# Moving three pieces of work around the choice of experts: 1/rms before the last rows, the first weight splits behind the choice, the first expert's tokens before the slot table

## The chip, the cores and the metric

One Trainium2 chip, one of its cores. The metric is device time in microseconds for one execution of the whole program (a mixer block, a mixture of experts, a second block with two feed-forward nets and two attentions). The change touches the stretch between the mixer's last projection and the first expert.

## The reference, cut to what matters

512 tokens of width 1024. After the mixer, `h = rms_norm(x)` goes into a mixture of 32 experts in 4 groups; each token takes two experts of one group, and each expert is a gated net of inner width 512.

```python
def hierarchical_moe(h, w_rg, b_rg, w_re, b_re, w_gate, w_up, w_down):
    g_logits = xt @ w_rg + b_rg                      # 4 groups
    g_sel = jnp.argmax(g_logits, axis=-1)
    g_w = softmax(g_logits)[g_sel]
    e_logits = (xt @ w_re + b_re)[group g_sel]       # 8 experts of that group
    top_v, top_i = lax.top_k(e_logits, 2)
    e_w = jax.nn.softmax(top_v, axis=-1) * g_w
    expert_id = g_sel * 8 + top_i
    ...                                              # tokens sorted by expert
    y = (jax.nn.silu(xb @ w_gate[e]) * (xb @ w_up[e])) @ w_down[e]
    out = out.at[sorted_tok].add(y * sorted_w)
```

## The kernel before, in words

Everything is float32. A dense product is made of three passes over operands that are split into a high and a low half: `mm3` (lines 257 to 259) multiplies low by high, high by low, and high by high. The split is `hilo`: ScalarE copies the rounded half (line 203), VectorE subtracts it from the source (line 204). Weights arrive by DMA into buffers of the pool `t8` (16 buffers of 1 MB), are split in pieces of 128x1024 into the pool `wp` (3 buffers), and a `t8` buffer is free for the next transfer once both of its pieces are split.

**Order.** A scheduler places each engine's instructions from the order of the program text and its own estimates; on its engine each then runs in the order written down. `keep_in_program_order` forbids it to move the marked instruction past others. The names in rows are tiles: `ps` is a PSUM bank, `t` any buffer of the shared pools, `wh` and `wl` the halves of a weight piece, `x` the residual stream.

**Into the experts.** `router` (line 556) returns `step(k)`, called for each of the 8 feature blocks of the new `x`: it squares the block into the sum `hsq` (lines 215 and 217), adds the block's product with the router's weights to the logits (line 573), scales and transposes the block (lines 576 and 579) and copies it to token rows (line 581). `moe` (line 661) then takes 1/rms of `hsq` (`rstd`: column sums by TensorE at line 286, line 315, the square root at line 268 and its refinement on VectorE), writes the token rows to `hrow` in DRAM, and chooses groups and experts (lines 693 to 727).

**Two fixed experts first.** 25 positions hold one or two experts each; positions 0 and 1 are always experts 0 and 1 (`NFIXED`), all later ones are ordered by how many tokens an expert got. For experts 0 and 1 the token lists are found without a table (`fixed`, lines 747 to 752) and their rows gathered from `hrow` on the GpSimd queue (line 1042); `fixed2` (line 758) adds their combine weights. All other experts need the slot table: VectorE computes each assignment's row (lines 785 to 794, the tile `dest`), eight indirect DMAs on the GpSimd queue scatter the assignments to `table` in DRAM (line 804), seven more read it back as `tabb`, `tab2` and `tab3` (lines 824 to 832), and the next gathers use those.

**The loop.** `features(n)` transposes gathered rows (line 1052 for a large position, with a split after it; line 954 for one or two small experts), `up` and `down` are the expert's products, `turn` the transpose between them, and the gather for position n+2 is issued while position n is worked on. Position 2 is a pair of small experts, so its rows come through `tab3` and its transposes are line 954. The raw weights of positions 0 and 1 are loaded ahead of the choice; those of the other positions are addressed by the ordered list `order`, through register loads on the sync queue (line 634) that precede its DMAs (line 238).

Of the kernel before, what the change touches and what calls it, by code (L numbers as in the profile page):

```python
# [7 lines left out]
F32 = mybir.dt.float32  # L8
# [3 lines left out]
ALU = mybir.AluOpType  # L12
# [4 lines left out]
T, D = 512, 1024  # L17
NT = T // 128
ND = D // 128
# [13 lines left out]
NFIXED, NBIG, NSMALL, CAP = 2, 6, 18, 64  # L33
# [4 lines left out]
SPLITS = 2  # L38
# [14 lines left out]
SEQ = sequence()  # L53
# [22 lines left out]
class Blocks:  # L76


    def __init__(self, tiles, n, w=512):
        self.tiles, self.n, self.w, self.per = tiles, n, w, 2048 // w  # L80
# [37 lines left out]
class Net:  # L118
    def __init__(self, tc, ctx, A, out):
        self.tc, self.nc, self.A, self.out, self.ctx = tc, tc.nc, A, out, ctx  # L120
        nc = self.nc
        ec = ctx.enter_context
        self.own = None
        self.const = ec(tc.tile_pool(name="const", bufs=1))
        self.p8 = ec(tc.tile_pool(name="p8", bufs=16))
        self.p4 = ec(tc.tile_pool(name="p4", bufs=4))
        self.p2 = ec(tc.tile_pool(name="p2", bufs=5))
        self.wp = ec(tc.tile_pool(name="wp", bufs=3))
        self.sm = ec(tc.tile_pool(name="sm", bufs=2))
        self.pp = ec(tc.tile_pool(name="pp", bufs=8, space=PSUM))  # L130
        self.dr = ec(tc.tile_pool(name="dr", bufs=1, space=DRAM))
        c = self.const
        self.x = c.tile([128, ND, T], F32, name="x")
        self.vec = c.tile([128, NV], F32, name="vec")
        nc.scalar.dma_start(self.vec, A["vec"])
        self.cc = c.tile([128, NC_], F32, name="cc")
        nc.scalar.dma_start(self.cc, A["cc"])
        self.ident = self.cc[:, C_ID:C_ID + 128]
        self.ones = c.tile([128, 128], F32, name="ones")
        nc.vector.memset(self.ones, 1.0)  # L140
        self.table = self.dr.tile([ROUNDS * 128 * NE, 4], I32, name="table")
        self.ordd = self.dr.tile([1, NE], I32, name="ordd")
        self.hrow = self.dr.tile([T, D], F32, name="hrow")
        self.pay = c.tile([128, NT, 2, 4], I32, name="pay")
        self.br = c.tile([128, NG + NE], F32, name="br")
        self.order = c.tile([128, NE], I32, name="order")
        self.payf = c.tile([128, NT, NFIXED, 4], F32, name="payf")
        self.payi = c.tile([128, NT, 2], F32R, name="payi")
        self.g12 = c.tile([128, ND], F32, name="g12")
        o1, o2 = VOFF["norm_final_g"], VOFF["g_ffn1_2"]  # L150
        nc.vector.tensor_tensor(self.g12, self.vec[:, o1:o1 + ND], self.vec[:, o2:o2 + ND], op=ALU.mult)
# [48 lines left out]

    def hilo(self, hi, lo, src):
        nc = self.nc
        nc.scalar.copy(hi, src)  # L203
        nc.vector.tensor_tensor(lo, src, hi.bitcast(F32), op=ALU.subtract)  # L204

    def half(self, hi, lo, src, g):

# [346 lines left out]
    def router(self):  # L554

        nc, W = self.nc, NG + NE
        self.root_table()
        x4 = self.t8([128, 2, D])
        nc.gpsimd.memset(x4, 0.0)
        self.xts = [x4[:, b, :] for b in range(2)]  # L560
        nc.gpsimd.dma_start(self.br, self.A["b_router"].partition_broadcast(128))
        wr = self.t2(ND * W).rearrange("p (k w) -> p k w", k=ND)
        nc.gpsimd.dma_start(wr, self.A["w_router"])
        for k in range(ND):
            nc.gpsimd.tensor_scalar(wr[:, k], wr[:, k], self.v("norm_ffn_g", k), None, op0=ALU.mult)
        self.lg = lg = self.ps()
        self.hsq = acc = self.t2()
        self.rows_x = rows = [self.t4([128, D]) for _ in range(NT)]

        def step(k):  # L570
            self.square(acc, self.x[:, k, :], k == 0)
            for i in range(NT):
                nc.tensor.matmul(lg[:, i * W:i * W + W], self.x[:, k, i * 128:i * 128 + 128], wr[:, k, :],
                                 start=k == 0 and i == 0, stop=k == ND - 1, skip_group_check=True)
            t = self.t2()
            nc.scalar.mul(t, self.x[:, k, :], self.v("norm_ffn_g", k))
            p = self.ps()
            for i in range(NT):
                nc.tensor.transpose(p[:, i * 128:i * 128 + 128], t[:, i * 128:i * 128 + 128], self.ident)
            for i in range(NT):  # L580
                nc.scalar.copy(rows[i][:, k * 128:k * 128 + 128], p[:, i * 128:i * 128 + 128])
        return step
# [78 lines left out]
    def moe(self):  # L661
        nc, A, tc = self.nc, self.A, self.tc
        mul, add, sub = ALU.mult, ALU.add, ALU.subtract
# [3 lines left out]
        ur, er = two[:, 0:128], two[:, 128:256]  # L667
        nc.gpsimd.tensor_copy(ur, self.cc[:, C_U:C_U + 128])
        nc.gpsimd.tensor_copy(er, self.ones)
        rt = self.rstd([self.hsq], D, "rtok")  # L670
        hrow, table, pay, payf = self.hrow, self.table, self.pay, self.payf
        for i in range(NT):
            nc.scalar.dma_start(hrow[i * 128:i * 128 + 128, :], rows[i])
# [5 lines left out]
        four = self.t2().rearrange("p (a i e) -> p a i e", i=NT, e=NE)  # L679
        where = {"Em": 0, "o1": 1, "o2": 2, "P": 3}  # L680

        def small(nm, w, dt=F32):
            return four[:, where[nm]] if nm in where else self.keep(nm, [128, NT, w], dt)
# [49 lines left out]
        for i in range(NT - 1):  # L733
            n = NT - i
            mm(rk[:, 32 * i + 32:160].rearrange("p (a e) -> p a e", e=NE), er,
               O[:, i:i + 1, :].to_broadcast([128, n, NE]), start=False, stop=i == NT - 2, skip_group_check=True)
        rk3 = rk[:, 0:128].rearrange("p (i e) -> p i e", e=NE)
# [16 lines left out]
        def fixed2(e):  # L754

            p = self.ps()
            for i in range(NT):
                mm(p[:, 0:2], sels[e].bitcast(F32)[:, i, :], payf[:, i, e, 0:2], start=i == 0, stop=i == NT - 1)
            nc.vector.tensor_copy(tabs[e].bitcast(F32)[:, 2:4], p[:, 0:2])
# [3 lines left out]
        rank, order, less = self.ranks(cn)  # L763
# [11 lines left out]
        nc.vector.tensor_tensor(pf[0], o1[:, :, fx], bc(ds, NFIXED), op=mul)  # L775
        nc.vector.tensor_tensor(pf[0], pf[0], pf[1], op=add)
        nc.vector.tensor_copy(pf[1], rt.rearrange("p (i o) -> p i o", o=1).to_broadcast([128, NT, NFIXED]))
        for e in range(NFIXED):
            fixed2(e)
        P = small("P", NE)  # L780
        rowr, row, tmp = P, Em, P

        def all4(t):
            return t.rearrange("p (o e) -> p o e", o=1).to_broadcast([128, NT, NE])
        nc.vector.tensor_tensor(rowr, rk3, all4(less), op=add)
        nc.vector.scalar_tensor_tensor(rowr, rowr, 127.5, all4(less), op0=ALU.is_ge, op1=mul)
        nc.vector.tensor_tensor(rowr, rowr, rk3, op=add)
        nc.vector.scalar_tensor_tensor(row, rowr, float(NE), all4(rank), op0=mul, op1=add)
# [13 lines left out]
        for i in range(NT):  # L802
            for j in range(2):
                ins = nc.gpsimd.indirect_dma_start(
                    table, bass.IndirectOffsetOnAxis(ap=dest[:, i, j:j + 1], axis=0),
                    pay[:, i, j, :], None, bounds_check=NR - 1, oob_is_err=False)
# [23 lines left out]
        for h in range(4):  # L830
            n = NE - NSMALL - h % 2
# [10 lines left out]
            else:  # L842
                self.gather(self.xts[n % 2][0:CAP], tabs[p][0:CAP])

        def features(n):
            xt = self.xts[n % 2]
            return self.expert_x(xt) if SEQ[n][0] < NBIG else self.small_x(xt)

        def up(n, xT, ys=()):
            unit = SEQ[n]  # L850
            tab = tabs[unit[0]]

            def also(k):
                if ys and k % 2:
                    for b in (k - 1, k):
                        self.add_block(ys, b)
            if unit[0] < NBIG:
                return self.expert_up(self.split_next, xT, tab, also)
            return self.small_up(unit, xT, tab, also)
# [4 lines left out]
        def down(n, aT):  # L864
# [3 lines left out]
            y = self.expert_down(self.split_next, aT, tab) if unit[0] < NBIG else self.small_down(unit, aT, tab)  # L868
            self.presplit(self.wnext + SPLITS)
            return [(t, sel) for t in y]  # L870
        a, ys = up(0, features(0)), ()
        xT = features(1)
        for n in range(NU - 2):
            aT = turn(n, a)
            gather(n + AHEAD)
            a = up(n + 1, xT, ys)
            xT = features(n + 2)
            ys = down(n, aT)
        aT, before = turn(NU - 2, a), ys
        ys = down(NU - 2, aT)  # L880
        a = up(NU - 1, xT, before)
# [10 lines left out]
    def spill(self, rounds, trow):  # L892
# [3 lines left out]
        with tc.For_i(1, nr, 1) as b:  # L896
            with tc.For_i(0, NE, 1) as p:
                A, B, C = (self.t8([128, 2048], dt) for dt in (F32R, F32, F32))
                P, Q = self.t2(), self.t2()
                G = self.t4([128, 1024], F32R)  # L900
                U, V = ([self.wp.tile([128, 2, 512], F32R, name=nm, tag=nm) for nm in ("wh", "wl")] for _ in range(2))
                X, Z = self.ps(), self.ps()
                self.own = {"t8": [A, B, C, B, C, B, C], "t4": [G, A[:, 0:D], A[:, D:2 * D]], "t2": [P, Q, G[:, 0:512]],
                            "w": [U, V] * 6, "ps": [X, Z, X, Z, X, X, Z] + [X, Z] * 4}
# [598 lines left out]
    def head_scores(self, score, bias, scale, rs):  # L1503
# [3 lines left out]
        where = [(0, 0), (1, 0), (0, 128), (2, 0)]  # L1507
        P = self.t8([128, 1280])
        mx = self.s("mx", [128, NT], bufs=4)
# [3 lines left out]
        def part(i):  # L1513
            return P[:, self.PO[i]:self.PO[i] + 128 * (i + 1)]
        for i in range(NT):
# [192 lines left out]
```

## Time and profile before

| | us |
|---|---|
| median of 3 runs | 2024.9 (2023.83 to 2028.1) |
| the profiled execution | 2022.01 |
| its span, first to last instruction | 2020.2 |
| TensorE busy | 1915.5 |
| VectorE busy | 1282.9 |
| ScalarE busy | 714.7 |
| GpSimd busy | 50.1 |

The profile describes one execution. A view of time gives start, duration, engine, line and operation, tiles written and read, and in brackets how long the engine was idle before it and what ended that. PEclk, the granted clock of TensorE, is a share of its higher level (1.00 is 2.4 GHz and 0.50 is 1.2 GHz). Matmuls are pipelined, so a busy TensorE isn't one at its peak.

### The profile page before, as it was taken

The numbers are of one execution on the slowest core, as the hardware profiler recorded it, in microseconds if no ns is written. First come the engines' busy times: TensorE is split into PE (matmuls) and PEld (weight loads), VectorE is DVE, ScalarE is ACT, GpSimd is POOL, SyncE is SP. The second block draws the span as 40 slices with busy tenths as digits, with TensorE's granted clock in tenths as the row PEclk, the third lists the DMA queues.
The fourth block names the chain that finished last, engine by engine and source line by source line (L and its number), as shares of the span: only waits on it lengthen the run. The fifth ranks groups of instructions, "written<-read, shape, count | busy, mean of one in ns | idle before, by whom it ended". The sixth has DMA issues, their size and how long they took to land.

```text
span 2020.2 us, 24426 instructions
## 1 busy us (share of the span) xinstructions
PE 1915.5 (95%) x9375; PEld 1428.0 (71%) x9375; DVE 1282.9 (64%) x2219; ACT 714.7 (35%) x1116; POOL 50.1 (2%) x69
## 2 busy tenths in 40 slices
PE   7999999988998999987999999999999999999997
PEld 5898888876554353332788888888877788888886
DVE  7999997547776576555754442359999655444323
ACT  5334335345333131111533222336367633323221
POOL 0000001003000000000000000000000000000000
PEclk9999999998999999999999999999999999999998
DMA  6121322537999999998222214240111122222311
GB/s 259 53 84 48 110 116 112 227 127 263 387 414 403 406 415 408 410 420 343 98 94 94 94 63 181 79 155 1 50 44 62 43 84 94 94 94 84 151 57 42
DMA packets 60087, 341.59 MB, mean 169 GB/s; under 512 B 8208, under 2 KB 9168, under 8 KB 27456
## 3 DMA queue, kind: packets, MB, share of 16 engines
q1 hardware_dynamic: 55152, 329.87, 42.2%
q0 software_dynamic: 3520, 6.35, 1.1%
q10 hardware_dynamic: 1296, 3.79, 0.5%
q8 instruction: 74, 1.21, 0.2%
q14 instruction: 45, 0.37, 0.1%
HBM read 339.37 MB, written 4.54 MB: 170 GB/s over the span
## 4 chain that ended last, share of the span: by engine, by line
PE 46%; DVE 3%; ACT 2%; issue 0%; DMA 0%; DVEq 0%; ACTq 0%; SPq 0%
PE ps L257 15%; PE ps L259 14%; PE ps L258 14%; PE ps L1549 1%; ACT t L1523 1%; DVE t L204 1%; PE ps L1536 1%; DVE wl L204 0%; ACT wh L203 0%; PE ps L1554 0%; DVE t L1458 0%; PE ps L1292 0%; ACT t L203 0%; DVE t L1329 0%; DVE t L1519 0%
## 5 line engine op out<-in xcount | busy, mean ns | idle before, releaser
L257 PE MATMUL ps<-t,wl 128*128 128x512 f32 x1728 | 685.0, 397 | 19.3 <-ACT t L208 18.8
L258 PE MATMUL ps<-t,wh 128*128 128x512 f32 x1728 | 681.7, 395 | 1.0 <-DVE t L209 1.0
L259 PE MATMUL ps<-t,wh 128*128 128x512 f32 x1728 | 682.0, 395 | 0.0
L203 ACT CAST wh<-t 128x1024 fp32r<-128x1024 f32 (+3 forms) x321 | 325.0, 1016 | 715.5 <-PE ps L259 532.7
L204 DVE TENSOR_TENSOR wl<-t,wh 128x1024 fp32r<-128x1024 f32 (+3 forms) x321 | 378.4, 1182 | 210.9 <-ACT wh L203 209.0
L257 PEld LDWEIGHTS ps<-t,wl 128*128 128x128 f32 x1728 | 325.8, 189 | 97.1 <-ACT t L208 19.6
L258 PEld LDWEIGHTS ps<-t,wh 128*128 128x128 f32 x1728 | 326.5, 189 | 76.7 <-DVE t L209 2.2
L259 PEld LDWEIGHTS ps<-t,wh 128*128 128x128 f32 x1728 | 325.7, 188 | 75.2
L257 PE MATMUL ps<-wh,t 128*128 128x256 f32 (+2 forms) x440 | 147.0, 336 | 23.2 <-DVE t L204 23.2
L972 PE MATMUL ps<-t,t 128*32 128x512 f32 (+1 forms) x832 | 161.1, 599 | 5.9 <-DMA t<-in_w_up 3.3
L403 DVE SCALAR_TENSOR_TENSOR t<-t,vec,t 128x512 f32<-128x512 f32 x240 | 165.5, 744 | 0.4
L1025 DVE TENSOR_TENSOR x<-x,ps 128x512 f32<-128x512 f32 x200 | 126.3, 682 | 46.3 <-PE ps L1024 45.4
L258 PE MATMUL ps<-wl,t 128*128 128x256 f32 (+2 forms) x440 | 145.5, 331 | 0.0
L259 PE MATMUL ps<-wh,t 128*128 128x256 f32 (+2 forms) x440 | 144.5, 328 | 0.0
L257 PEld LDWEIGHTS ps<-wh,t 128*128 128x128 f32 x440 | 85.5, 194 | 33.0 <-DVE t L204 25.1
L972 PEld LDWEIGHTS ps<-t,t 128*32 128x32 f32 (+1 forms) x832 | 41.2, 122 | 90.7 <-issue 76.5
L1181 DVE TENSOR_TENSOR t<-ps,rbc 128x512 f32<-128x512 f32 x44 | 30.4, 690 | 115.6 <-PE ps L259 115.6
L259 PEld LDWEIGHTS ps<-wh,t 128*128 128x128 f32 x440 | 85.5, 194 | 7.4
L1024 PEld LDWEIGHTS ps<-t,t 128*128 128x128 f32 x248 | 43.0, 191 | 67.2 <-issue 31.6
L258 PEld LDWEIGHTS ps<-wl,t 128*128 128x128 f32 x440 | 85.6, 195 | 6.8
L1024 PE MATMUL ps<-t,t 128*128 128x512 f32 x248 | 78.8, 424 | 11.5 <-DVE t L1012 7.4
L1178 DVE TENSOR_TENSOR t<-ps,rbc 128x512 f32<-128x512 f32 x44 | 30.3, 690 | 81.8 <-PE ps L259 81.6
(315 smaller groups left out, 1613.7 us busy)
## 6 DMA issues: line engine op xcount, KB each, us to landing
t<-in_w_down SPq DMA_DIRECT2D x80, 1024.0 KB, 17.9
t<-in_w_gate SPq DMA_DIRECT2D x64, 1024.0 KB, 19.6
t<-in_w_up SPq DMA_DIRECT2D x64, 1024.0 KB, 19.7
t<-in_w_in SPq DMA_DIRECT2D x24, 1024.0 KB, 4.8
t<-in_w_gate SPq DMA_DIRECT2D x44, 512.0 KB, 3.5
t<-in_w_up SPq DMA_DIRECT2D x44, 512.0 KB, 3.5
t<-in_w_down SPq DMA_DIRECT2D x8, 768.0 KB, 5.2
t<-in_w_qi SPq DMA_DIRECT2D x4, 1040.0 KB, 6.0
```

Of the source, the lines that this page charges most:

```text
L203: nc.scalar.copy(hi, src)
L204: nc.vector.tensor_tensor(lo, src, hi.bitcast(F32), op=ALU.subtract)
L257: mm(acc, a[1], b[0], start=first, stop=False)
L258: mm(acc, a[0], b[1], start=False, stop=False)
L259: mm(acc, a[0], b[0], start=False, stop=last)
L403: nc.vector.scalar_tensor_tensor(y[c], src, w, y[c], op0=mul, op1=add)
L972: nc.tensor.matmul(p[o:o + c, :], xT[:, k * CAP + i:k * CAP + i + c], w[:, q, :], start=k == 0, stop=k == ND - 1)
L1024: self.nc.tensor.matmul(p, yT[:, k * 128:k * 128 + 128], sel, start=j == 0, stop=j == n - 1)
L1025: self.nc.vector.tensor_tensor(self.x[:, k, :], self.x[:, k, :], p, op=ALU.add)
L1178: nc.vector.tensor_tensor(t, accs[0], rbc, op=mul)
L1181: nc.vector.tensor_tensor(a, accs[1], rbc, op=mul)
L1523: nc.scalar.activation(part(i), part(i), AF.Exp, bias=nm[:, i:i + 1], scale=scale, accum_out=su[:, i:i + 1])
```

## The change

1. `step` takes 1/rms right after the last block's square is added, in the text ahead of the last block's transposes, and `moe` only picks it up.
2. The first two weight pieces of expert 0 are split by an explicit `presplit(SPLITS)` after the choice of experts; `pin` keeps both instructions of each split in program order, so they can't be moved ahead into the mixer.
3. `features(0)`, which transposes and splits expert 0's tokens, stands ahead of the slot table, and the table's first VectorE instruction keeps its program order.

```diff
     def hilo(self, hi, lo, src):
         nc = self.nc
-        nc.scalar.copy(hi, src)
-        nc.vector.tensor_tensor(lo, src, hi.bitcast(F32), op=ALU.subtract)
+        pin = self.pin or (lambda ins: ins)
+        pin(nc.scalar.copy(hi, src))
+        pin(nc.vector.tensor_tensor(lo, src, hi.bitcast(F32), op=ALU.subtract))
...
             self.square(acc, self.x[:, k, :], k == 0)
+            if k == ND - 1:
+                self.rt = self.rstd([acc], D, "rtok")
...
-        rt = self.rstd([self.hsq], D, "rtok")
+        rt = self.rt
...
+        self.pin = tc.keep_in_program_order
+        self.presplit(SPLITS)
+        self.pin = None
         for e in range(NFIXED):
             fixed2(e)
+
+        def features(n):
+            xt = self.xts[n % 2]
+            return self.expert_x(xt) if SEQ[n][0] < NBIG else self.small_x(xt)
+
+        xT = features(0)
...
-        nc.vector.tensor_tensor(rowr, rk3, all4(less), op=add)
+        tc.keep_in_program_order(
+            nc.vector.tensor_tensor(rowr, rk3, all4(less), op=add))
...
-        a, ys = up(0, features(0)), ()
+        a, ys = up(0, xT), ()
```

The lines of the changed kernel lie up to 14 further down than those of before. What moves is best seen in the order of each engine. On TensorE, at the end of the mixer: before, the last block's transposes (line 579) stand ahead of the column sums (line 286).

```order
L573 MATMUL ps_3003<-t2_2993,x_78 128x36 x4
L579 MATMUL ps_3384<-cc_81,t2_3382 128x128 x4
L573 MATMUL ps_3003<-t2_2993,x_78 128x36 x4
L579 MATMUL ps_3402<-cc_81,t2_3400 128x128 x4
L286 MATMUL ps_3419<-ones_83,t2_3004 128x2 x4
L731 MATMUL ps_3481<-O_3479,ur_3415 128x128
```

The same place in the changed kernel, where the column sums are line 288 and the transposes line 583:

```order
L577 MATMUL ps_3003<-t2_2993,x_78 128x36 x4
L583 MATMUL ps_3384<-cc_81,t2_3382 128x128 x4
L577 MATMUL ps_3003<-t2_2993,x_78 128x36 x4
L288 MATMUL ps_3397<-ones_83,t2_3004 128x2 x4
L583 MATMUL ps_3419<-cc_81,t2_3417 128x128 x4
L735 MATMUL ps_3481<-O_3479,ur_3432 128x128
```

Only this pair changes places; the rest of TensorE's order is the same in both kernels. On VectorE before, from the fixed experts' combine weights (`tabf1`) into the slot table, whose first row is line 785:

```order
L936 TENSOR_SCALAR own_3516<-cc_81,rp_3520 32x32
L941 CAST order_90<-ps_3523 128x32
L943 COPY rank_3527<-ps_3523 128x32
L759 COPY tabf0_3496<-ps_3547 128x2
L944 TENSOR_SCALAR less_3528<-rank_3527 128x32
L945 TENSOR_SCALAR lesst_3529<-rank_3527 128x32
L759 COPY tabf1_3508<-ps_3553 128x2
L946 TENSOR_TENSOR less_3528<-less_3528,lesst_3529 128x32
L785 TENSOR_TENSOR t2_3444<-ps_3481,less_3528 128x128
```

The same place in the changed kernel; line 206 is VectorE's half of a split, here of weight pieces (`wl`) and of expert 0's tokens (`t8_3567`), and the slot table begins at line 799:

```order
L206 TENSOR_TENSOR wl_3548<-t8_3009,wh_3547 128x1024
L951 CAST order_90<-ps_3523 128x32
L953 COPY rank_3527<-ps_3523 128x32
L206 TENSOR_TENSOR wl_3552<-t8_3011,wh_3551 128x1024
...
L763 COPY tabf1_3508<-ps_3561 128x2
L206 TENSOR_TENSOR wl_3663<-t8_3009,wh_3662 128x1024
L206 TENSOR_TENSOR t8_3567<-ps_3568,t8_3567 128x512
L206 TENSOR_TENSOR t8_3567<-ps_3575,t8_3567 128x512
L799 TENSOR_TENSOR t2_3444<-ps_3481,less_3528 128x128
```

Three weight pieces that VectorE split during the mixer before now stand here, and expert 0's two token splits stand ahead of the slot table. Further on before, the two rows of `dest` (line 794), which the scatters wait for, stand around the first token split, and the fourth weight piece (`wl_3669`) comes after all of the table:

```order
L693 TENSOR_REDUCE rr1_3569<-t2_3444 128x4
L819 TENSOR_TENSOR cm_3600<-cm_3600 128x1
L204 TENSOR_TENSOR t8_3626<-ps_3627,t8_3626 128x512
L794 CAST dest_3563<-rr1_3569 128x4
L818 TENSOR_SCALAR cm_3600<-cm_3600 128x1
L204 TENSOR_TENSOR t8_3626<-ps_3634,t8_3626 128x512
...
L821 CAST rounds_3613<-cm_3600 128x1
L204 TENSOR_TENSOR wl_3669<-t8_3011,wh_3668 128x1024
```

In the changed kernel the table's end reads as follows, with `dest` at line 808:

```order
L697 TENSOR_REDUCE rr0_3588<-t2_3444 128x4
L829 TENSOR_REDUCE cm_3623<-ce_3624 128x1
L206 TENSOR_TENSOR wl_3669<-t8_3011,wh_3668 128x1024
L808 CAST dest_3586<-rr0_3588 128x4
...
L697 TENSOR_REDUCE rr1_3592<-t2_3444 128x4
L833 TENSOR_TENSOR cm_3623<-cm_3623 128x1
L206 TENSOR_TENSOR wl_3685<-t8_3013,wh_3684 128x1024
L808 CAST dest_3586<-rr1_3592 128x4
```

The fourth weight piece now stands ahead of the first row of `dest`, and the fifth ahead of the second row.

## Rows read from the trace of the kernel before

**Rows 1.** Windows: busy time of engines, granted clock, DMA share, GB/s by stretch.

```profile
490.00:535.00 45.00, 41.17 (x210) 27.74 (x208) 35.35 (x51) 22.31 (x26) 3.25 (x4) 0.92 1.01 404
535.00:545.00 10.00, 10.00 (x63) 6.83 (x65) 7.75 (x15) 3.73 (x4) 0.94 (x1) 1.00 0.79 289
545.00:945.00 400.00, 363.01 (x1824) 161.26 (x1816) 253.69 (x453) 87.70 (x113) 17.82 (x18) 0.97 1.01 411
```

**Rows 2.** Timeline of TensorE, end of the mixer to the first expert.

```profile
444.14 1.36 PE L286 MATMUL ps<-ones,t 128*128 128x2 f32 x8
...
460.16 3.57 PE L758 MATMUL ps<-payf,t 128*128 128x2 f32 x16
463.59 1.95 PE L1052 MATMUL ps<-cc,t 128*128 128x128 f32 x8
467.41 0.80 PE L257 MATMUL ps<-wh,t 128*128 128x512 f32 x1 [1.87 <-DVE t L204]
```

**Rows 3.** Timeline of VectorE, same stretch.

```profile
443.02 0.69 DVE L217 TENSOR_TENSOR t<-t,t 128x512 f32<-128x512 f32 x1 [0.31 <-ACT t L215]
...
460.27 0.19 DVE L941 CAST order<-ps 128x32 int32<-128x32 f32 x1 [1.15 <-PE ps L939]
...
462.06 0.16 DVE L759 COPY tabf<-ps 128x2 f32<-128x2 f32 x1 [1.51 <-PE ps L758]
...
463.77 0.16 DVE L759 COPY tabf<-ps 128x2 f32<-128x2 f32 x1 [1.37 <-PE ps L758]
...
466.00 0.17 DVE L794 CAST dest<-rr 128x4 int32<-128x4 f32 x1
...
466.67 0.68 DVE L204 TENSOR_TENSOR t<-ps,t 128x512 fp32r<-128x512 f32 x1
...
471.46 1.23 DVE L204 TENSOR_TENSOR wl<-t,wh 128x1024 fp32r<-128x1024 f32 x1 [2.74 <-ACT wh L203]
```

**Rows 4.** Timeline of ScalarE, same stretch.

```profile
464.72 0.59 ACT L203 CAST t<-ps 128x512 fp32r<-128x512 f32 x1 [12.46 <-PE ps L1052]
...
470.38 1.05 ACT L203 CAST wh<-t 128x1024 fp32r<-128x1024 f32 x1 [4.21 <-PE ps L259]
```

**Rows 5.** Timeline of GpSimd: first scatter, gather for position 2.

```profile
466.47 1.06 POOL L804 DMA_INDIRECT table<-pay,dest  x1 [5.16 <-DVE t L792]
...
489.08 1.09 POOL L1042 DMA_INDIRECT t<-hrow,tab  x1 [5.55 <-PE ps L259]
```

**Rows 6.** DMA issues 488 to 490, then 495 to 497: us from issue to landing.

```profile
t<-hrow,tab POOLq DMA_INDIRECT x1, 5.9
...
t<-hrow,tab POOLq DMA_INDIRECT x1, 7.6
```

**Rows 7.** DMA issues of the whole run, the gathers for positions 0 and 1.

```profile
t<-hrow,tabf POOLq DMA_INDIRECT x2, 3.3
```

**Rows 8.** Timeline of TensorE at position 2's transposes.

```profile
495.18 0.71 PE L954 MATMUL ps<-cc,t 64*128 64x64 f32 x8
```

**Rows 9.** Timeline of TensorE after a stall at 521, and twelve matmuls on.

```profile
524.66 0.80 PE L257 MATMUL ps<-wh,t 128*128 128x512 f32 x1 [3.83 <-DVE t L204]
...
529.90 1.09 PE L1024 MATMUL ps<-t,t 128*128 128x512 f32 x4
```

**Rows 10.** Windows around that stall (columns as in rows 1).

```profile
520.00:523.00 3.00, 0.83 (x6) 0.33 (x5) 2.77 (x4) 3.00 (x6) 0.00 (x0) 1.00 1.05 426
523.00:529.80 6.80, 5.14 (x12) 4.08 (x13) 4.79 (x11) 1.29 (x2) 0.00 (x0) 0.50 1.01 419
```

**Rows 11.** Timeline of the sync queue, weight DMAs before the dry stretch.

```profile
529.96 0.34 SPq L238 DMA_DIRECT2D t<-in_w_up  x1
537.08 1.71 SPq L238 DMA_DIRECT2D t<-in_w_down  x2
```

**Rows 12.** DMA issues 529 to 531, 537 to 538: us to landing.

```profile
t<-in_w_up SPq DMA_DIRECT2D x1, 1024.0 KB, 9.8
...
t<-in_w_down SPq DMA_DIRECT2D x1, 1024.0 KB, 5.2
```

More of the change, by code (lines that the diff above doesn't have):

```diff
@@ L777, in moe @@
         nc.vector.tensor_copy(pf[1], rt.rearrange("p (i o) -> p i o", o=1).to_broadcast([128, NT, NFIXED]))
+        self.pin = tc.keep_in_program_order
+        self.presplit(SPLITS)
+        self.pin = None
         for e in range(NFIXED):
             fixed2(e)
+        def features(n):
+            xt = self.xts[n % 2]
+            return self.expert_x(xt) if SEQ[n][0] < NBIG else self.small_x(xt)
+        xT = features(0)
         P = small("P", NE)
@@ L843, in gather @@
                 self.gather(self.xts[n % 2][0:CAP], tabs[p][0:CAP])
-        def features(n):
-            xt = self.xts[n % 2]
-            return self.expert_x(xt) if SEQ[n][0] < NBIG else self.small_x(xt)
         def up(n, xT, ys=()):
```

## The prediction

> **What bounds the kernel now.** Three views matter, and I read them from coarse to fine.
>
> The first is busy time by stretch [rows 1]. From 545 to 945 us the DMA engines are at 1.01 of their time and move 411 GB/s: this is the stream of expert weights, and TensorE, at 363.01 of 400 us, is not what sets its pace. So the end of the experts is set by when that stream was last short of work. That stretch is in the rows too: from 490 to 535 it is full (1.01), from 535 to 545 it stands at 0.79, so 2.1 us of ten are lost. A transfer needs a free `t8` buffer, buffers come free as pieces are split and multiplied, and around 537 they come too late. Whatever shifts TensorE's work before 537 shifts the stream, and through it the whole run. Whatever is gained or lost behind 545 is swallowed as long as the stream stays full.
>
> The second is the timeline of the four engines from 443 to 472 [rows 2 to 5]. Here the change acts. The reader is to see who waits: TensorE idles 1.87 us ahead of the first expert's first matmul at 467.41, for VectorE's split of expert 0's tokens at 466.67, while ScalarE had its half of it ready at 464.72 + 0.59 = 465.31. VectorE was busy with the slot table. The split was 1.36 us late, and the wait is real.
>
> The third is position 2's transposes at 495.18 [rows 8]. They read rows that the slot table's tables had to fetch. There is no idle time in that row, but hardly any slack either: the gather was issued at 489.08 [rows 5] and landed 5.9 us later [rows 6], at 494.98. In the kernel before, the slot table is in time by 0.2 us.
>
> **The change part by part.**
>
> *1/rms ahead of the last transposes.* The column sums wait for the sum of squares, complete at 443.02 + 0.69 = 443.71 [rows 3], but start at 444.14 behind the transposes [rows 2]. In the new order they can start some 0.06 later than 443.71, so 0.37 us earlier, and the choice of experts moves up by that. The transposes and the four writes of `hrow` behind them become later by about the 1.36 us of the column sums less the 0.37; only the gathers read them, and those wait for the choice of experts and the token lists first, so this is free. If something else holds the chain, the gain is nothing; bounds 0 and 0.37.
>
> *Three weight splits behind the choice.* They leave the mixer, where other work hid them, so their removal gives nothing. They come in at 1.23 us each [rows 3], 3.7 us of VectorE time, at a place where VectorE idled 1.15, 1.51 and 1.37 us waiting for TensorE [rows 3], 4.0 in all. I take nothing for them; at worst the ordering rows behind one of them come 0.1 to 0.5 us later. ScalarE's halves run in its long idle time of 12.46 us [rows 4].
>
> *Expert 0's tokens ahead of the table.* TensorE's transposes at 463.59 follow `fixed2` (460.16 + 3.57) [rows 2]; that stays. Behind them ScalarE's half ends at 465.31 less up to 0.2, VectorE's low half follows at once (0.68), and the first matmul starts at about 465.9 in place of 467.41: 1.5 us earlier, bounds 1.36 (only the queueing goes) and 1.73 (all of the 0.37 arrives too). These matmuls run at the lower clock, as they did before, so at the end of expert 0 some of this is left: I take 1.0.
>
> *The slot table behind them.* This is the cost. The table's ten or so rows now follow the token splits, and the first row of `dest` follows the fourth weight piece. That piece waits for TensorE: its ScalarE half started at 470.38 [rows 4], when six matmuls had used up the first piece, and its VectorE half ended at 471.46 + 1.23 = 472.69 [rows 3], that is 5.28 us after the first matmul. From 465.9 this gives 471.2, and `dest` (0.17) is there at 471.4 in place of 466.17. The table is 5.2 us later. If the six matmuls ran at the full clock it would be 1.3 less (rows 9 give 0.44 us each at half clock), so 3.9 to 5.2. Behind `dest` on GpSimd's queue stand eight scatters, seven reads and the gather for position 2. From the first scatter at 466.47 to that gather at 489.08 is one chain of issues and landings [rows 5], and I move it as a whole: gather at 494.3. The gather for position 3 is now ahead of it on that queue, but it needs only the first table read and fits into the wait for the others.
>
> *What is late next.* The gather lands 5.9 us on, at 500.2; the next one took 7.6 [rows 6], so up to 501.9. TensorE reaches position 2's transposes at about 494.2 and idles 6 us; it goes on 5.0 us later than before. Its order is the same in both kernels, so nothing can fill the gap, and VectorE's splits for the down weights are queued behind the copy of those transposes. After a shorter stall of 3.83 us at 521 the granted clock was 0.50 (1.2 GHz) until 529.8 [rows 10], and the twelve matmuls that followed took 529.90 - 524.66 = 5.2 us [rows 9], 2.6 more than at 2.4 GHz. I charge the same 2.6 here. TensorE's path from 500 to 537 is then 5.0 + 2.6 = 7.6 us late.
>
> *What of it reaches the end.* At 537.08 the sync queue issues a transfer that waited for a buffer; the one before, issued at 529.96, lands 9.8 later at 539.8 [rows 11, 12]. So 2.7 us of work were still queued. A release that comes 7.6 us later costs the stream between 7.6 - 2.7 = 4.9 and 7.6. The transfer of 537.08 took only 5.2 us to land, close to a free queue, but those behind it were still building one up, so I take a value near the lower end, 5.5.
>
> **Sum.** 2022.01 (the profiled execution, span 2020.2) + 5.5 = 2027.5; the median of the runs shown is 2.9 above that execution, so 2024.9 + 5.5 = **2030.4 us**, 0.27% slower. A measurement of this kernel can tell about 0.2%, 4 us, from no change.
>
> **The rivals.**
>
> *The other side: no stall, a little faster.* If the gather lands before TensorE asks for it, only the gains stay. It decides at one point: the rows must land by 494.2, so the first scatter would have to start 0.8 us earlier than at 466.47. For it speaks that most of the 22.6 us from scatter to gather [rows 5] are landings, which vary with the traffic. Against it stands the order itself, in which `dest` can't come ahead of a piece that needs six matmuls. The stream would gain the 1.0 us that expert 0 gains: 2023.9. I give it 15%.
>
> *The stall is there but mostly hidden.* The clock does not fall, and all 2.7 us that are queued at 537 count: 5.0 - 2.7 = 2.3, which gives 2027.2. Against it: the shorter stall of rows 9 did lower the clock. 13%.
>
> *The table's DMAs are quicker than before.* With the transfers to hidden buffers starved, the gather finds an emptier queue. For positions 0 and 1, with no weights moving, it took 3.3 us for twice the rows [rows 7]. With 3.3 in place of 5.9 the stall shrinks by 2.6: 5.5 - 2.6 = 2.9, so 2027.8. Against it: at 490 to 535 the stream is full [rows 1], and the buffers that expert 1 frees keep it going. 14%. The Trainium skill (DMA: Bandwidth & Descriptors, section Anatomy of one DMA, SWDGE path) prices a GpSimd DMA at 2.0 us plus its bytes at 436 GB/s, an estimate of 2.6 us for 64 rows of 4 KB; by that the sum would be 5.5 - 3.3 = 2.2. The trace disagrees at this very place, with 5.9 us.
>
> **How the numbers follow.** The forecast has 52%, the rivals 15, 13 and 14; 6% are left for what I don't see. The range goes from the rival on the other side, with the whole 1.5 us at its best, 2023.4, to the forecast with the 7.6 us gather (1.7 more) and all of the lateness passed on (2.1 more), 2034.2. The forecast alone would be 2027.5 to 2034.2. Faster by over 0.2% needs 4 us, and the two gains together hold under 2: 5%. Slower by over 0.2% takes most of the forecast and a little of the rest: 49%. The other two rivals and the one on the other side lie within: 46%.
>
> **What would show it.** Right: the column sums start ahead of the last transposes; the first expert's first matmul comes about 1.5 us earlier with nearly no idle time ahead of it; the first scatter is about 5 us later; TensorE idles about 6 us ahead of line 964 (954 before) and the granted clock is 0.50 there; the DMA share between 535 and 550 falls below 0.79; the last down weights come about 5 us later. Wrong: the transposes of position 2 without idle time ahead of them, or the stream full again by 545 with the weights ending where they did. The step that I trust least is how much of a late TensorE the queued transfers absorb.

## The result, and the profile after

The changed kernel takes 2035.8 us (median of 5, 2032.65 to 2038.4) where the kernel before took 2023.83 on the same chip: a ratio of 1.0055 (1.0044 to 1.0065). That is 11 us slower by the ratio and 12 by the medians. The profiled execution took 2032.65 us with a span of 2030.9; it was the shortest of the five. The forecast was 2030.4 with a range up to 2034.2, so the direction was right and the loss about twice what I had worked out.

The front of the chain went as forecast. TensorE's timeline from the column sums to position 2 (start, duration, then the instruction, and in brackets the idle time before it):

```profile
443.99 1.05 PE L288 MATMUL ps<-ones,t 128*128 128x2 f32 x8 [1.29 <-DVE t L219]
...
465.66 0.79 PE L259 MATMUL ps<-wh,t 128*128 128x512 f32 x1 [0.55 <-DVE t L206]
...
501.99 1.11 PE L964 MATMUL ps<-cc,t 64*128 64x64 f32 x8 [7.41 <-DMA t<-hrow,tab]
...
503.04 0.79 PE L259 MATMUL ps<-wh,t 128*128 128x512 f32 x1
...
510.31 0.60 PE L1093 MATMUL ps<-cc,t 128*128 128x128 f32 x4
```

The first matmul comes 1.75 us earlier than in [rows 2], with 0.55 us of idle time in place of 1.87. Position 2's transposes come 6.8 us later than in [rows 8], behind a stall of 7.41 us, and the row says for what: the gathered rows. The last row stands right behind expert 0's down products, 8.32 us after the transposes; before, the same stretch ran from 495.18 to 501.50, in 6.32, with no idle time in either. The granted clock is 0.50 from 499.75 to 506.58. So the lower clock behind the stall costs 2.0 us, and TensorE is 8.8 us late at 510.

VectorE's timeline shows where the gather's lateness starts, and what queued behind the stall:

```profile
469.70 1.23 DVE L206 TENSOR_TENSOR wl<-t,wh 128x1024 fp32r<-128x1024 f32 x1 [1.34 <-ACT wh L205]
470.85 0.16 DVE L808 CAST dest<-rr 128x4 int32<-128x4 f32 x1
...
503.14 0.69 DVE L967 COPY t<-ps 128x512 f32<-128x512 f32 x1 [6.95 <-PE ps L964]
...
507.08 1.23 DVE L206 TENSOR_TENSOR wl<-t,wh 128x1024 fp32r<-128x1024 f32 x1 [1.91 <-ACT wh L205]
```

`dest` stands behind the fourth weight piece and is there 4.85 us later than in [rows 3]. On GpSimd the first scatter and the gather for position 2 follow, and the sync queue has a weight transfer that waits for the split of 507.08. That split waits in turn for ScalarE's half, which stood idle for a free split buffer (the second fence):

```profile
471.30 1.05 POOL L818 DMA_INDIRECT table<-pay,dest  x1 [9.71 <-DVE t L806]
...
493.36 1.66 POOL L1052 DMA_INDIRECT t<-hrow,tab  x1 [2.40 <-DMA tab<-table]
```

```profile
506.00 1.05 ACT L205 CAST wh<-t 128x1024 fp32r<-128x1024 f32 x1 [10.21 <-PE ps L261]
...
495.56 0.33 SPq L240 DMA_DIRECT2D t<-in_w_up  x1
508.33 3.45 SPq L240 DMA_DIRECT2D t<-in_w_down  x2
```

The sync queue issues nothing for 12.8 us. The windows show what that does to the stream (columns as in [rows 1]):

```profile
495.00:500.00 5.00, 0.00 (x0) 0.00 (x0) 1.20 (x2) 0.79 (x1) 0.01 (x1) 0.98 0.96 351
500.00:505.00 5.00, 3.01 (x13) 2.51 (x14) 1.86 (x4) 0.00 (x0) 0.94 (x1) 0.50 0.97 376
505.00:510.00 5.00, 5.00 (x20) 4.02 (x19) 3.09 (x8) 2.98 (x3) 0.00 (x0) 0.84 0.29 55
...
540.00:545.00 5.00, 5.00 (x23) 4.06 (x22) 4.48 (x5) 2.94 (x3) 0.00 (x0) 1.00 0.68 262
545.00:550.00 5.00, 5.00 (x23) 3.84 (x21) 2.83 (x5) 0.90 (x2) 0.00 (x0) 1.00 0.66 231
545.00:945.00 400.00, 366.91 (x1833) 165.97 (x1835) 258.27 (x462) 90.11 (x116) 17.83 (x19) 0.96 1.01 407
```

There are now two dry stretches. The first is new: 505 to 510, right behind the stall, where the stream stood at 1.01 before. It leaves the stream 6.0 us late: the transfer that landed at 537.31 before lands at 543.27. The second is the one of [rows 1], 8 us later and deeper: 0.68 and 0.66 from 540 to 550. There the transfer that left at 537.08 before [rows 11] leaves at 545.12, and the one ahead of it lands 7.5 us after its issue, at 546.0:

```profile
538.50 0.34 SPq L240 DMA_DIRECT2D t<-in_w_up  x1
545.12 0.33 SPq L240 DMA_DIRECT2D t<-in_w_down  x1
```

Behind it the stream is about as late as TensorE, and stays so while it is full: the same weight transfer lands at 564.4 in place of 555.7, and one at the end of the experts at 942.2 in place of 933.3, 8.7 and 8.9 us late. The rest of this execution's loss, 2 us, arises in the second block's attention between 1355 and 1520, where the granted clock is 0.97 after and 0.99 before. It isn't the change's: the traces of two runs below, part 1 alone and the kernel before with its reads reordered, have 0.97 there too, and lose 0.3 and 0.6 us by their medians. So it is the profiled execution of before that was a short one.

### The profile page after: what moved, and what is told of

Same layout as the page of the kernel before. It is cut to its first block, busy times and chain, and to the rows that moved or that the text cites. A ratio compares the mean times of both kernels' runs of the same rounds, so it can differ in the third digit from the quotient of the medians.

```text
span 2030.9 us, 24427 instructions
## 1 busy us (share of the span) xinstructions
PE 1923.8 (95%) x9375; PEld 1433.4 (71%) x9375; DVE 1282.9 (63%) x2219; ACT 714.5 (35%) x1116; POOL 49.4 (2%) x69
## 4 chain that ended last, share of the span: by engine, by line
PE 46%; DVE 3%; ACT 2%; issue 0%; DMA 0%; DVEq 0%; ACTq 0%; SPq 0%
PE ps L259 15%; PE ps L261 14%; PE ps L260 14%; PE ps L1559 1%; ACT t L1533 1%; DVE t L206 1%; PE ps L1546 1%; DVE wl L206 0%; ACT wh L205 0%; PE ps L1564 0%; DVE t L1468 0%; PE ps L1302 0%; ACT t L205 0%; DVE t L1339 0%; DVE t L1529 0%
## 5 line engine op out<-in xcount | busy, mean ns | idle before, releaser
L1034 PE MATMUL ps<-t,t 128*128 128x512 f32 x248 | 78.7, 424 | 12.1 <-DVE t L1022 8.0
```

The lines of the kernel that those rows point to most:

```text
L1034: self.nc.tensor.matmul(p, yT[:, k * 128:k * 128 + 128], sel, start=j == 0, stop=j == n - 1)
```

## The experiments

Each was compared with runs of the kernel before on its own chip, whose medians were 2025.36, 2024.72 and 2024.85 us in the three groups of four.

**A late table and nothing else, twice.** The kernel before, with copies that delay the scatters (14, and 5):

```diff
+        for q in range(14):
+            nc.gpsimd.tensor_copy(wide[1 - q % 2], wide[q % 2])
+        dest = wide[0][:, 0:2 * NT].rearrange("p (i j) -> p i j", j=2)
```

> The kernel before, with fourteen dependent GpSimd copies of 128x128 (0.29 us each in the trace of before) between the rows of dest and the first scatter; nothing else moves. They start when the second row of dest is there (467.27 in the trace of before), so the first scatter comes at about 471.4, as late as in the changed kernel (471.30). Theory 1, the late slot table is the whole loss and almost all of TensorE's delay reaches the stream: gather for position 2 lands at about 500 to 502, TensorE idles 5 to 7 us ahead of position 2's transposes, the stream runs nearly dry around 505 to 510, and the run is 9 to 13 us slower than before, since this kernel lacks the 1.7 us that the changed one gains at the first matmul. Theory 2, my prediction's step that queued transfers absorb 2 us or more: 5 to 6 us slower. Theory 3, the moved splits or the lost cover in the mixer cause the loss: within 2 us of before.

> The same with five copies: first scatter about 2.3 us later than in before, at 468.8. Theory 1: the slack of 0.2 us is used up, TensorE idles 2 to 4 us at position 2's transposes, with the lower clock behind it, and the run is 3 to 7 us slower than before. Theory 2 (queued transfers absorb 2 us or more): 0 to 3 us slower. Theory 3: no difference. Against the run with fourteen copies it shows how much each us of lateness costs.

With 14 copies: 2040.57 us, 1.0074 (1.0057 to 1.0091), 15 us slower, where theory 1 had put 9 to 13. With 5: 2031.45 us, 1.0035 (1.0022 to 1.0048), 6 us slower, within its 3 to 7. So a late table alone makes a loss of this size, without any moved split. The copies took 0.42 us each, so the first scatters came at 473.99 and 470.19, later than meant. TensorE at position 2, with 14 and with 5:

```profile
506.67 1.09 PE L959 MATMUL ps<-cc,t 64*128 64x64 f32 x8 [11.75 <-DMA t<-hrow,tab]
```

```profile
500.36 0.68 PE L959 MATMUL ps<-cc,t 64*128 64x64 f32 x8 [4.00 <-DMA t<-hrow,tab]
```

**The order of `dest` mended.** The changed kernel with the table's instructions up to `dest`, and expert 0's splits, kept in program order:

```diff
+            keep(nc.vector.tensor_copy(dest[:, :, j:j + 1], rr))
...
+        self.pin = tc.keep_in_program_order
         a, ys = up(0, xT), ()
+        self.pin = None
```

> The changed kernel with its one VectorE order mended: the slot table's instructions up to dest and the splits of expert 0's weights keep program order, so that dest stands behind expert 0's token splits but ahead of every further weight piece. dest then comes at about 467.4, some 1.4 us later than in before and 3.5 earlier than in the changed kernel, while the first matmul keeps its 1.7 us. Theory 1: stall of about 2 us at position 2 instead of 7.4, and a time 5 to 8 us below the changed kernel, 0 to 4 above the kernel before. Theory 3 (splits and cover): as the changed kernel, 11 us above before.

2034.62 us, 1.0047 (1.003 to 1.0064): 9 us slower, where I had expected 0 to 4. `dest` did come early, at 467.89. But the table was no earlier for it. GpSimd's timeline, first to last scatter and the gather:

```profile
468.35 1.05 POOL L820 DMA_INDIRECT table<-pay,dest  x1 [7.18 <-DVE t L807]
469.71 1.91 POOL L820 DMA_INDIRECT table<-pay,dest  x1 [0.30 <-issue]
471.92 1.94 POOL L820 DMA_INDIRECT table<-pay,dest  x1 [0.30 <-DVE wl L206]
474.16 1.25 POOL L820 DMA_INDIRECT table<-pay,dest  x1 [0.30 <-issue]
...
479.99 1.43 POOL L820 DMA_INDIRECT table<-pay,dest  x1 [0.30 <-issue]
...
495.27 1.63 POOL L1056 DMA_INDIRECT t<-hrow,tab  x1 [2.42 <-DMA tab<-table]
```

The first scatter is 2.95 us earlier than in the changed kernel, the last only 0.65, since two of them come 2.2 us behind the one before, where the changed kernel has 1.3 to 1.4. That last one lands at 486.17 (485.23 in the changed kernel), and the gather at 503.74. The chain behind `dest` doesn't move as a whole. What sets its landings was the next question.

**The weights held back until the table is written.** The changed kernel, with a DMA of 16 bytes on the sync queue ahead of one weight transfer:

```diff
+            if self.wat == 16:
+                self.tc.keep_in_program_order(
+                    self.nc.sync.dma_start(self.keep("held", [1, 4], I32), self.table[0:1, :]))
             self.wraw[nm, p, h] = self.load8(
```

> The changed kernel with one added tiny DMA on the sync queue that reads a row of the slot table; it stands ahead of the weight transfer issued at 476.74, so that transfer and all behind it wait until the eight scatters have landed. Theory 1 (each DMA of the table lands behind the weight transfers that were issued ahead of it): the last scatters land 2 to 3 us after their issue in place of 4.6 to 6, so the table is written at about 483 in place of 485.2; the four reads of tab3 land at 487 to 490, the gather for position 2 at 494 to 499 in place of 501.95, and the stall falls from 7.4 us to 0 to 4. The stream is idle from 478 to 484, which costs some of it back; I expect 0 to 6 us below the changed kernel. Rival (scatters and reads take as long by themselves): the table's landings stay, the stall stays 7.4 us, and the held stream adds up to 4 us to the changed kernel's time.

2030.86 us, 1.0033 (1.002 to 1.0045), 6 us slower than before and by the medians some 5 faster than the changed kernel; the two profiled executions are only 1.6 us apart. DMA issues from 470 to 490 (the last figure is the median us from issue to landing):

```profile
tab<-table POOLq DMA_DIRECT2D x2, 12.0 KB, 2.0
tab<-table POOLq DMA_DIRECT2D x2, 7.0 KB, 1.8
tab<-table POOLq DMA_DIRECT2D x2, 6.5 KB, 2.6
...
tabb<-table POOLq DMA_DIRECT2D x1, 12.0 KB, 1.9
t<-hrow,tabb POOLq DMA_INDIRECT x1, 10.6
t<-hrow,tab POOLq DMA_INDIRECT x1, 11.9
```

With the stream silent (its windows stand at 0.20 and 0.02 from 475 to 485), the last three scatters land 2.1 to 2.3 us after their issue, against 4.6 to 5.6 in the changed kernel, and six of the seven reads in 1.8 to 2.0 against 3.2 to 5.3. So what makes the table's DMAs slow is the weights in flight, and theory 1 holds there. The stall did not shrink, though, and that part of my expectation missed: the gather, issued at 489.20 just behind three released transfers, took 11.9 us and TensorE still waited 7.27. The released transfers were all still queued at the stall, and from 500 to 510 the DMA share stays at 1.01, where it was 0.97 and 0.29. But this run doesn't show that queued transfers absorb a stall, since the hold itself had set the stream back: the transfer that landed at 537.31 before lands at 543.75, 6.4 us late, with 6.0 in the changed kernel. Its last weights are 7.0 us late, with 8.9 there. The Trainium skill (DMA: Bandwidth & Descriptors, section Anatomy of one DMA, SWDGE path) gives a GpSimd DMA a fixed 2.0 us; these reads agree with it when nothing else moves.

**Position 2's reads first, and its transposes later.** The changed kernel with `tab3` read ahead of `tabb` and `tab2`; with the transposes behind expert 0's down products; with both; and the kernel before with the reads reordered. The second edit:

```diff
             a = up(n + 1, xT, ys)
-            xT = features(n + 2)
+            if n:
+                xT = features(n + 2)
             ys = down(n, aT)
+            if not n:
+                xT = features(n + 2)
```

> The changed kernel with the seven reads of the slot table in another order: the four of tab3, which position 2's gather waits for, come first, then tabb, then tab2. The gather for position 2 is then issued at about 490.5 in place of 493.36 and ahead of that for position 3. Theory 1 (the loss is the late gather at position 2): with 6 to 8.6 us to land, TensorE's stall of 7.4 us falls to 2 to 4.5, and the run is 3 to 7 us faster than the changed kernel, that is 5 to 8 above before. Rival (the loss is elsewhere, in the splits): no change against the changed kernel, 11 above before.

> The changed kernel with one move in the loop: position 2's transposes, and the copy behind them on VectorE, follow expert 0's down products instead of standing ahead of them. The slot table stays as late as in the changed kernel. Expert 0's down products (about 5.5 us at the higher clock) then fill most of the wait, and VectorE's splits of the down weights are no longer queued behind the copy. Theory 1: stall of 1 to 2.5 us, no dry stretch at 505 to 510, 6 to 10 us faster than the changed kernel, within 4 us of before. Theory 3: as the changed kernel, 11 us above before.

> The changed kernel with both mendings: tab3 read first, and position 2's transposes behind expert 0's down products. In the run with the late transposes alone, the gather took 11 us because five weight transfers were issued around it; issued at 490.5 it stands ahead of three of them. Theory 1: it lands at 497 to 500, when TensorE is at about 499.5; stall 0 to 1 us, no dry stretch at 505 to 515, and the time within 3 us of before, on either side, with the first matmul still 1.7 us earlier. If the rows still land behind 502, the weights that are queued ahead of it set its landing, and the run stays 3 to 6 above before. Rival: 11 above before.

> The kernel before with tab3 read first, as a control: there is no stall at position 2 to take away, so the same time as before within 3 us. If it is faster by more, the kernel before lost time at the later gathers too.

Reads first: 2032.88 us, 1.0039 (1.0024 to 1.0055), 8 us slower, at the edge of what I expected, and not by the way that I expected: the reads of `tab3` landed at 491.15 to 493.73, the gather left at 493.23, hardly earlier than in the changed kernel (493.36), and the stall was 8.10. Transposes later: 2031.61 us, 1.0032 (1.002 to 1.0043), 6 us slower, where I had expected at most 4. TensorE went on with the down products, whose transfers (issued at 497.82 and 500.88) kept the stream busy, and the gather took 11 us. So the stall stayed, and the dry stretch only came later: the DMA share is 0.96 from 505 to 510 and 0.10 from 510 to 515. Its transposes:

```profile
505.61 1.11 PE L967 MATMUL ps<-cc,t 64*128 64x64 f32 x8 [6.30 <-DMA t<-hrow,tab]
```

Both together: 2027.52 us, 1.0014 (1.0005 to 1.0023), 3 us slower; the stall is 3.58 us, where I had expected 0 to 1, and the stream is dry nowhere from 495 to 510. This takes back 8 of the 11 us with the splits and the order of `dest` as in the changed kernel, so the rival can hold no more than the 3 us that are left. The control is at 2025.36 us, 1.0002 (0.9993 to 1.0012): its gather lands at 492.89, 2 us earlier than before, and with no stall there that is worth nothing.

**Work in the stall.** The changed kernel with matmuls on constants in the idle time:

```diff
+                for q in range(32):
+                    tc.keep_in_program_order(nc.tensor.matmul(
+                        p[:, 0:256], self.two[:, 0:128], self.two, start=True, stop=True, skip_group_check=True))
             xT = features(n + 2)
```

> The changed kernel with 32 added matmuls of 128x256 on constants in the stall, ahead of position 2's transposes; their result is not used. TensorE is then busy from 494.6 to about 501.5 and the granted clock should stay at 1.00 where it was 0.50 from 499.75 to 506.58. The gather and the wait for it stay. If the lower clock behind the stall is 2.6 to 3.4 us of the loss and passes on to the stream, the run is 2 to 3.5 us faster than the changed kernel; if only the stall counts, it is as the changed kernel within 1.

2036.08 us, 1.0059 (1.0045 to 1.0072), as the changed kernel, but inconclusive: the added matmuls ended at 498.5, the gather took 11 us this time, TensorE idled 6.68 us behind them, and the clock fell to 0.50 all the same, from 503.15 to 509.98. What the clock costs is in the rows above (2.0 us); that it can be saved was not shown.

**The parts alone.** Parts 1 and 2, here against the changed kernel; part 3; part 1:

```diff
-        xT = features(0)
         P = small("P", NE)
...
-        a, ys = up(0, xT), ()
+        a, ys = up(0, features(0)), ()
```

> Parts 1 and 2 of the change alone: 1/rms early and the first weight splits pinned behind the choice; expert 0's tokens stay behind the table in the text. In VectorE's order the fourth weight piece again stands ahead of the first row of dest and the fifth ahead of the second. Theory 1 (whatever puts dest behind a weight piece makes the table late): first scatter at 469 to 472, stall of 4 to 9 us at position 2, 5 to 12 us above before. Rival (part 3, the token splits ahead of the table, is what costs): within 2 us of before.

> Part 3 alone: expert 0's tokens ahead of the slot table, with the table's first instruction pinned; 1/rms and the weight splits as before. VectorE's order again has the fourth weight piece ahead of the first row of dest. Theory 1: first scatter at about 471, stall of 6 to 9 us, 8 to 13 us above before, the same as the whole change. Rival (the pinned weight splits cost): within 2 us of before.

> Part 1 alone: 1/rms ahead of the last transposes. dest stays ahead of the weight pieces. My prediction counts 0.37 us for it: the column sums start at about 0.1 to 0.4 us earlier, and the time is within 2 us of before.

Parts 1 and 2: 2037.24 us, 1.0063 (1.0047 to 1.008). Part 3: 2036.04 us, 1.0054 (1.0037 to 1.007). Part 1: 2025.16 us, 1.0001 (0.9991 to 1.0011). Nearly all as theory 1 had it: the first loses 12.4 us where it allowed 12, and the stalls of the first two, 11.97 and 10.48 us, were longer than I had said. The pinned splits and the early tokens each put `dest` behind a weight piece, so each alone costs what both cost. Part 1 alone shows why a gain in front is worth nothing here:

```profile
466.75 0.79 PE L257 MATMUL ps<-wh,t 128*128 128x512 f32 x1 [1.87 <-DVE t L204]
...
495.13 0.68 PE L956 MATMUL ps<-cc,t 64*128 64x64 f32 x8 [0.68 <-DMA t<-hrow,tab]
```

The first matmul is 0.66 us earlier than in [rows 2], and TensorE then waits 0.68 us for the gather and starts at 495.13, where it had started before. The gather left 1.61 us earlier, at 487.47, and still landed at 494.99, where it had landed at 494.96: its landing didn't move with its issue.

**All kernels with one loop order, together.** Lateness is against the profiled execution of before: of position 2's transposes (495.18 there), of TensorE right behind expert 0's down products (501.50), and of a weight transfer right behind the last of the experts (issued at 935.85). "Loss" is the median less that of before on the same chip.

| kernel | transposes late, us | TensorE late behind them | last weights late | loss, us |
|---|---|---|---|---|
| part 1 alone | -0.05 | -0.1 | 0.0 | 0.3 |
| before, `tab3` first | 0.5 | 0.5 | 1.5 | 0.6 |
| five copies | 5.2 | 6.7 | 6.6 | 6.1 |
| weights held | 6.0 | 7.5 | 7.0 | 6.0 |
| `tab3` first | 6.5 | 9.3 | 9.5 | 8.2 |
| the change | 6.8 | 8.8 | 8.9 | 12.0 |
| `dest` first | 8.6 | 11.1 | 10.8 | 9.3 |
| part 3 alone | 8.7 | 11.7 | 12.7 | 11.2 |
| matmuls in the stall | 10.0 | 12.1 | 11.5 | 11.4 |
| parts 1 and 2 | 10.8 | 13.5 | 13.6 | 12.4 |
| fourteen copies | 11.5 | 13.8 | 13.7 | 15.2 |

The two columns in the middle agree within 1 us, whatever made TensorE late: the stream absorbs 0.6 us of it at most. The loss follows them within 1.5 us, except for the changed kernel, whose median lies 3.1 above; its profiled execution was the shortest of its five, and the others have no trace. No version beat the kernel before.

## Why the prediction was wrong, step by step

*1/rms and the weight splits:* right in size, in part by luck. TensorE's products of `fixed2` start at 459.73 in place of 460.16, 0.43 earlier (0.37 forecast). But the column sums start only 0.15 earlier, since the sum of squares is complete at 443.94 in place of 443.71; the rest comes from their taking 1.05 us in place of 1.36. And the kernel before with its reads reordered, which has the same code up to here, starts `fixed2` at 459.87, so 0.3 us is the spread between executions. The three splits in that stretch cost no more than that.

*Expert 0's tokens:* right. First matmul at 465.66, forecast 465.9; the gain of 1.75 us is at the upper bound.

*The slot table:* right in place and size as far as `dest` (470.85, forecast 471.4). "I move it as a whole" was wrong as a rule. Here it erred little, since the gather's issue moved by 4.3 us where `dest` moved by 4.85; but the run with `dest` mended shows that landings behind weight transfers, not `dest` alone, set that time.

*The gather:* mis-sized. It took 8.59 us to land where I had taken 5.9 and allowed 7.6, and the stall was 7.41 in place of 6. The rival of quicker DMAs had it the wrong way round: the DMA share was 0.96 from 495 to 500, and across the runs with a stall this gather took 8.1 to 11.9 us. Its comparison was also misread: the gathers of [rows 7] fill tiles of twice the rows, but from 455 to 463, with both of them in it, the GpSimd queue moved only 0.15 MB, which is some 18 rows of 4 KB each.

*The clock:* right in kind, 2.0 us where I had charged 2.6. TensorE's path was 8.8 us late, forecast 7.6.

*What of it reaches the end:* this is the step that failed. I let transfers that are queued at 537 [rows 11, 12] absorb 2.1 of TensorE's 7.6 us, and up to 2.7. They absorbed nothing: TensorE was 8.8 us late behind the stall and the last weights 8.9. Two things were wrong.

First, a queue of 2.7 us was hardly a reserve. On the empty queue at 508.33 in the changed kernel a transfer takes 4.8 us to land, and in a full stream, at the 411 GB/s of [rows 1], one of 1024 KB takes 2.55; so by my estimate a transfer must leave 2.25 us ahead of the landing before it for the stream to lose nothing, and 0.45 of the 2.7 was to spare. [Rows 12] hinted at it: 5.2 us for the transfer of 537.08 is close to an empty queue, as I wrote, and I took the lower end all the same. The run with both mendings tests the step by itself. There the stream had no dry stretch at the stall and was 0.5 us late ahead of this release; the release came 2.38 us late, at 539.46, and the last weights were 4.1 us late.

Second, I had not seen that the changed kernel's stream runs dry at the stall itself. The chain is in the rows: the copy of line 967 keeps VectorE waiting until 503.14; the second weight split behind it (507.08) also waits for TensorE, now at half clock, to use up a piece, since there are three `wp` buffers; and the transfer that needs that `t8` buffer leaves at 508.33, where it had left at 499.95. The transfer issued ahead of it, at 495.56, lands at 506.55, so the queue stood empty. This set the stream back by 6.0 us, so that at the release of 545.12 only 0.9 us was queued in place of 2.7. With 8.8 for 5.5, my sum would have been 2033.7, with no term for absorption.

*What is left open:* the 2 us between 2033.7 and the measured 2035.8. The 8.9 us of late weights by themselves lie inside the range, whose upper end is 9.3 above the median I started from. The other four executions of the changed kernel are 3 to 6 us longer than the profiled one, and why is not known, since they have no trace.

## What to carry to other kernels

When an instruction that starts a long chain of DMAs moves behind a weight split on its engine, price the chain to the first instruction that needs its last result, under the traffic that will run beside it, and not by the shift of its first link. Ask then what stands behind that waiting instruction on every engine, down to the buffers whose release issues the next transfers: a stall there can empty the stream on the spot. Queued transfers cover a late release only as far as it still comes early enough for its own transfer to start up; here that took 2.25 of the 2.7 us that were queued. Where two paths meet with no slack, as TensorE and the gather did here, a gain on one alone is worth nothing; nor is a gather that leaves earlier, if its landing is set by the transfers around it.

## What the runs showed of the hardware

A small GpSimd DMA that landed in about 2 us on quiet DMA engines (1.8 to 2.0 for six of the seven reads with the weights held) took up to 7.35 us under the weight stream (the first scatter of the same run), and a gather into a tile of 64 rows of 4 KB up to 11.9. A weight transfer of 1024 KB landed 4.8 us after its issue on an empty queue. The scatters of one kernel are not evenly spaced: 2.2 us for two of them with `dest` first, 1.3 to 1.4 throughout the changed kernel, though VectorE splits weight pieces beside them in both; no run shows what sets it.
